# Rotary heads of a float32 network: queries stacked as a high and a low part on 128 partitions, masked scores by two rounded products

## The chip, the cores and the metric

The kernel runs on one core of one Trainium2 chip, as one launch. The metric is the device time of that core in microseconds (us). Three runs of the kernel before took 1568.48, 1573.48 and 1576.81 us; their median, 1573.48 us, is the time before.

## The reference, cut to what matters

A network of four layers over 256 tokens of 1024 features, all in float32. The last two layers hold the attentions with rotary embedding that the change is about:

- In the third layer eight heads of 64 features attend in a window of 128 tokens (`sliding_window_sink_attention`). Their eight queries share two heads of keys, four queries to a head, and both queries and keys are rotated (`apply_rope`). A second set of eight heads (`forgetting_attention`) is not rotated.
- In the fourth layer sixteen rotated heads share four rotated heads of keys (`dsa_attention`). Each query attends to the 64 keys that an index of eight small heads scores highest; the index has rotated queries and one rotated key head of its own.

```python
def apply_rope(t, cos, sin):
    half = t.shape[-1] // 2
    tf = t.astype(jnp.float32)
    t1, t2 = tf[..., :half], tf[..., half:]
    return jnp.concatenate([t1 * cos - t2 * sin, t2 * cos + t1 * sin], axis=-1).astype(t.dtype)
...
        s = jnp.einsum('bqhgd,bqthd->bhgqt', qi, ks, preferred_element_type=jnp.float32) * scale
        s = jnp.where(sel_valid[:, None, None], s, -jnp.inf)
        p = jax.nn.softmax(s, axis=-1)
        o = jnp.einsum('bhgqt,bqthd->bqhgd', p.astype(v.dtype), vs)
```

## The kernel before, in words

The 256 tokens are two tiles of 128, called m = 0 and m = 1. Nearly all products are of a split form: a float32 number is written as a rounded float32r number (high part, by ACT, L260 for weights) plus the rounded rest (low part, by DVE, L261), and `mm3` (L276 to L279) adds three rounded products of 128 rows, high by high, high by low and low by high. Weights are loaded from HBM by SP's queue into four buffers `raw` (L235), split into the buffers `wh` and `wl`, and used by `tok_out` (L368, tokens on the partitions of the result) or `feat_unit` (L384, features on them).

The stages run in the order of `todo` (L1371): gMLP, FFN, chunk attention, FFN, `even_mix` (L901), its FFN, `dsa` (L1020), mixture of experts. Within and across these the tile framework places the instructions on the queues of the engines, so that products of the next part stand between the small steps of an attention. Each engine then works its queue in that order. The order in `dsa` is set by the string `ORD = "cq0123"` (L44): c is `choose` (L1042), the selection of keys for both token tiles; q is the second half of the queries (`query(1)`, L1081); 0 to 3 are the four groups of four heads (`group`, L1090). `query(0)` and the products for values stand ahead of these. Groups 0 and 1 take their sums from the four PSUM buffers `d`, groups 2 and 3 from the two buffers `m` (L1107).

`attend` (L666) handles a group of four heads. It has four chains, one for each token tile and each pair of heads, and `together` issues their steps in turn. A chain does: the scores of two heads into one PSUM buffer (L678 to L682), the largest of a row (DVE, L697 or L700), the exponential with its sum (ACT, L709, into a buffer `s2`, of which there are four), the transposes (PE, L716), the copy of these (ACT, L719), the product with the values (PE, L724) and the division (DVE, L728, L729). Keys reach to the end of the query's own tile, so a head has 128 keys for m = 0 and 256 for m = 1. For the rotated heads the mask is added by the tensor engine: a rounded product of 128 rows of the identity with the mask (L681) opens the sum, and the score (L682), one float32 product over the 64 features of the head, closes it. Each L682 appears in the profile as two instructions. Heads that are not rotated have no L681; their bias is added by DVE.

`rotate` (L831) makes the rotary embedding of a tile of tokens on DVE: a product with the cosine (L837), two with the sine (L838, L839) and the sum (L841, or L845 twice with the heads of the keys doubled), in buffers `rt`. `tr_copy` (L848) transposes the result, 128 columns at a time (PE, L853), and copies it out (ACT, L854). Two heads lie in each block of 128 columns, so an even head ends on partitions 0 to 63 and an odd head on 64 to 127 (`half`, L736); keys are doubled so that both find them. `ev_sq` (L924) and `ev_kv` (L912) do this in `even_mix`, `ev_iq`, `ev_ki` and `ev_q` (L1030, L1035, L1084) in `dsa`.

`keep` buffers that matter here: six of `a8` and two of `xn`, each given out in turn. `fox_bias` (L965) loads a small table into an `xn` buffer (L968).

Of the kernel before, what the change touches and what calls it, by code (L numbers as in the profile page):

```python
# [16 lines left out]
P = 128  # L17
# [31 lines left out]
# ---------------------------------------------------------------- layouts  # L49


def _rows(w, kk):
    """[K, N] -> [K/(128*kk), 128, kk*N]: row-chunk units, kk chunks of 128 rows each."""
    K, N = w.shape
    return w.reshape(K // (P * kk), kk, P, N).transpose(0, 2, 1, 3).reshape(K // (P * kk), P, kk * N)


def _a_units(w, cols=256):
    """[1024, N] -> [N/cols, 128, 8*cols]: all of K for a block of columns."""
    K, N = w.shape  # L60
    return w.reshape(K // P, P, N // cols, cols).transpose(2, 1, 0, 3).reshape(N // cols, P, (K // P) * cols)


def _b_units(w, cols=512):
    """[1024, N] -> [(N/cols)*2, 128, 4*cols]: half of K for a block of columns."""
    K, N = w.shape
    return (w.reshape(2, K // (2 * P), P, N // cols, cols).transpose(3, 0, 2, 1, 4)
            .reshape((N // cols) * 2, P, (K // (2 * P)) * cols))


def _fm(v):
    """vector [n*128] -> [128, n], entry n*128+p at (p, n)."""
    return v.reshape(-1, P).T
# [5 lines left out]
def _layout(i):  # L79
# [46 lines left out]
    # small vectors, feature-major, side by side  # L126
# [13 lines left out]
    # small vectors, one row  # L140
# [3 lines left out]
    # constants of the shapes alone  # L144
# [14 lines left out]
def tile_net(ctx: ExitStack, tc: tile.TileContext, a: dict, out: bass.AP):  # L159
# [36 lines left out]
    def xn_():  # L196
        return t_keep("xn", D, 2)
# [4 lines left out]
    # ------------------------------------------------------------ constants  # L202
# [29 lines left out]
    # ------------------------------------------------------------ weights  # L232
# [31 lines left out]
    def unit(src, k, where=None, loaded=None):  # L264
        """a unit of k chunks of 128 rows -> for each chunk its two parts [128, columns]."""
# [22 lines left out]
    def together(*chains):  # L288
        """issue the steps of independent chains in turn"""
# [4 lines left out]
    # ------------------------------------------------------------ norms  # L294
# [54 lines left out]
    def norm(m, outs, r=None):  # L349
        """token tile m of the norms outs: (xh, xl, gain row) or (xh, xl, A, B), feature-major"""  # L350
# [33 lines left out]
    def feat_unit(xt, w, psx=None):  # L384
        """feature-major product of one unit of 256 columns -> psum [128, 2, 256]."""
# [8 lines left out]
    def feat_tile(xt, w, ps, m, psx):  # L394
        """token tile m of feat_unit, token-major first."""
# [10 lines left out]
    def feat_pair(xt, ws, psx):  # L406
        """feat_unit of the units ws, one token tile after the other."""
# [25 lines left out]
    def add_rows(d, th, tl, w, first, last, ms=(0, 1), cs=(0, 1)):  # L433
        """one chunk of 128 rows of a down projection into the four sums d[m][c]."""
# [5 lines left out]
    def finish(d, tail, g=None):  # L440
        """the chunks of the tail, one token tile after the other, then h += (g *) sums and its squares."""
# [15 lines left out]
    def out_proj(oT, src, g=None, order=(0, 1, 2, 3)):  # L457
        """h += (g *) o @ w for oT = (oh, ol) feature-major; two chunks of rows per unit."""
# [13 lines left out]
    # ------------------------------------------------------------ modulation  # L472
# [11 lines left out]
    def ada_step(n=1):  # L484
        """the next 256 entries of a modulation: their columns of the weights lie on the partitions"""
# [16 lines left out]
    def mod_scale(nm, i, gain):  # L502
        """(1 + sc) * gain, feature-major."""
# [4 lines left out]
    def spread(v):  # L508
        """feature-major [128, 8] -> [128, 1024], the same row on every partition."""
# [10 lines left out]
    # ------------------------------------------------------------ gated MLPs  # L520
# [69 lines left out]
    # ------------------------------------------------------------ gMLP mixer  # L590
# [74 lines left out]
    # ------------------------------------------------------------ softmax attention  # L665
    def attend(q, kT, vv, mask, oT, g, psx, sinks=None, cumq=None, rmask=None):  # L666
        """heads 4g..4g+3 of 16: q(h) and kT(h) feature-major [64, 256], vv(h, kb) [128, 64], mask(m, pair)
        added to the scores, or rmask(m) by the tensor engine; the result feature-major in oT."""
        ob = g2().rearrange("p m (h d) -> p m h d", h=4)

        def chain(m, hh):
            nk = (m + 1) * P
            ms = slice(m * P, (m + 1) * P)
# [4 lines left out]
            for i, hd in enumerate(pair):  # L678
# [3 lines left out]
                PE.matmul(ps[:, sl], q(hd)[:, ms], kT(hd)[:, 0:nk], start=rmask is None, stop=True)  # L682
# [56 lines left out]
    # ------------------------------------------------------------ chunk attention  # L739
# [17 lines left out]
    def chunk_attn():  # L757
        xk, xq = ahead[2]
        oT = new_xt()
        for j in range(4):  # L760
# [19 lines left out]
            def mask(m, pair):  # L780
# [3 lines left out]
            attend(lambda hd: half(qT, hd - 4 * j), lambda hd: half(kT, hd - 4 * j),  # L784
                   lambda hd, kb: vv[:, kb, (hd - 4 * j) * 64:(hd - 4 * j + 1) * 64], mask, oT, j,
# [45 lines left out]
    def rotate(ps, m, nh, dup=1):  # L831
        """rotary embedding of token-major heads [128, nh*64], each written dup times."""
        n = nh * 64
        t1, t2, o = (t_part("rt", 512, lay["rt"])[:, 0:w] for w in (n, n, n * dup))
# [5 lines left out]
        if dup == 1:  # L840
# [7 lines left out]
    def tr_copy(src, dst, m, scale=1.0):  # L848
        """token-major [128, n*128] -> dst [128, n, 256] at token tile m."""
# [7 lines left out]
    # ------------------------------------------------------------ even layer  # L857
# [21 lines left out]
    def x0_norm(m, gain, xs, rs):  # L879
        """h = x0, the normed h, and its own norm."""  # L880
# [20 lines left out]
    def even_mix():  # L901
        xt = ahead[2]
        kvb = a8()
        skT = kvb[:, 0:512].rearrange("p (k t) -> p k t", k=2)
        sv = kvb[:, 512:768].rearrange("p (m d) -> p m d", m=2)
        lf = kvb[:, 768:784].rearrange("p (m d) -> p m d", m=2)
        cum = kvb[:, 784:800].rearrange("p (m d) -> p m d", m=2)
        sqT = kvb[:, 1024:2048].rearrange("p (k t) -> p k t", k=4)
# [3 lines left out]
        def ev_kv(m, c, ps):  # L912
            tr_copy(rotate(ps[:, 0:128], m, 2, dup=2), skT, m)
# [10 lines left out]
        def ev_sq(m, c, ps):  # L924
            tr_copy(rotate(ps, m, 8), sqT, m, scale=0.125)
# [15 lines left out]
        fv = a8()[:, 0:1024].rearrange("p (m d) -> p m d", m=2)  # L941
# [23 lines left out]
        def fox_bias(j):  # L965
            """for the heads of group j, minus the sums of the keys' columns, causal"""
# [17 lines left out]
        def fox(j, cbs):  # L984
# [6 lines left out]
            attend(lambda hd: half(fqT, hd - 4 * j), lambda hd: half(fkT, hd - 4 * j),  # L991
# [408 lines left out]
```

## Time and profile before

| | us |
|---|---|
| median of three runs | 1573.48 |
| the three runs | 1568.48, 1573.48, 1576.81 |
| span of the profiled execution, first to last instruction | 1564.6 |
| PE busy in it | 1503.8 |
| DVE busy | 1206.7 |
| ACT busy | 940.9 |

The table holds the times and the first part of the page. The profiled execution has no time of its own on record beside its span; what lies around the span (launch and end) is in the runs' times and not in the span, and the median is 8.9 us above it. Starts of instructions are in us from the beginning of the span. A matmul's shown duration runs to the end of its pipeline, and one begins while the last one ends; what a stream of them costs is read from start to start. PEclk 1.00 is 2.4 GHz and 0.50 is 1.2 GHz; a mean between the two is a mixture.

### The profile page before, as it was taken

The page shows a single profiled execution, that of the slowest core. Times are in us where ns is not written, and L with a number is a line of the kernel's source. Part 1 is how long each engine was busy: PE and PEld are TensorE (multiplying, and loading weights), DVE is VectorE, ACT ScalarE, POOL GpSimd, SP SyncE. Part 2 cuts the span into 40 slices and gives each one's busy share as a digit, 9 for nine tenths or more (in the row PEclk, how much of TensorE's full clock was granted, in tenths as well). Part 3 has the DMA queues.
Part 4 walks back from the last instruction along what each step waited for, and adds up shares of the span by engine and source line. Part 5 has one row for each costly group of instructions (what it writes and reads, how often), then busy time and mean ns, then how long its engine had stood idle before and what let it go on. Part 6 is the DMA issues. An engine that isn't in the chain of part 4 may idle for free. (4 is left out here: it accounts for less than half of the span.)

```text
span 1564.6 us, 23309 instructions
## 1 busy us (share of the span) xinstructions
PE 1503.8 (96%) x9000; PEld 1307.1 (84%) x9000; DVE 1206.7 (77%) x2039; ACT 940.9 (60%) x1567; POOL 15.6 (1%) x26
## 2 busy tenths in 40 slices
PE   6999999999999999999899999999899999999996
PEld 5888998899799898878799997867688888888875
DVE  6688877765798887846888866844688888888996
ACT  7565555565575555645644444535487777777774
POOL 0000000000000000000000000000000000000000
PEclk9999999999999999989999999959899999999998
DMA  8567676364388662532698961510379998899894
GB/s 312 207 226 285 238 249 218 126 233 142 137 314 282 232 240 83 204 120 82 219 356 311 335 226 44 186 54 28 121 274 334 336 334 310 327 349 331 288 354 152
DMA packets 54150, 359.85 MB, mean 230 GB/s; under 512 B 6400, under 2 KB 6656, under 8 KB 15632
## 3 DMA queue, kind: packets, MB, share of 16 engines
q1 hardware_dynamic: 54032, 358.30, 63.6%
q8 instruction: 72, 1.18, 0.3%
q14 instruction: 46, 0.38, 0.1%
HBM read 357.23 MB, written 1.05 MB: 229 GB/s over the span
## 5 line engine op out<-in xcount | busy, mean ns | idle before, releaser
L261 DVE TENSOR_TENSOR wl<-raw,wh 128x1024 fp32r<-128x1024 f32 (+4 forms) x342 | 363.7, 1070 | 85.2 <-ACT wh L260 83.8
L260 ACT ACTIVATE wh<-raw 128x1024 fp32r<-128x1024 f32 (+4 forms) x342 | 315.1, 932 | 145.0 <-DMA raw<-in_fin_dram 41.0
L261 DVE TENSOR_TENSOR wlx<-raw,whx 128x1024 fp32r<-128x1024 f32 (+2 forms) x231 | 258.7, 1123 | 44.1 <-ACT whx L260 43.2
L260 ACT ACTIVATE whx<-raw 128x1024 fp32r<-128x1024 f32 (+2 forms) x231 | 224.2, 976 | 51.4 <-PE m L278 14.7
L277 PE MATMUL d<-wh,a 128*128 128x512 f32 (+4 forms) x448 | 167.7, 376 | 6.1 <-ACT a L343 6.1
L278 PE MATMUL d<-wl,a 128*128 128x512 f32 (+4 forms) x448 | 167.0, 374 | 0.9 <-DVE wl L261 0.9
L279 PE MATMUL d<-wh,a 128*128 128x512 f32 (+4 forms) x448 | 166.0, 371 | 0.2 <-DVE a L346 0.2
L278 PE MATMUL m<-a,wh 128*128 128x256 f32 x496 | 142.5, 287 | 0.0
L277 PE MATMUL m<-a,wh 128*128 128x256 f32 x496 | 141.9, 286 | 0.0
L279 PE MATMUL m<-a,wl 128*128 128x256 f32 x496 | 141.7, 286 | 0.0
L492 DVE SCALAR_TENSOR_TENSOR raw<-raw,silu_c 128x1024 f32<-128x1024 f32 x96 | 116.1, 1219 | 6.2 <-DMA raw<-in_e_ada_dram 2.9
L277 PE MATMUL d<-a,th 128*128 128x512 f32 x264 | 106.6, 404 | 2.8 <-ACT th L549 2.8
L278 PE MATMUL d<-a,th 128*128 128x512 f32 x264 | 104.4, 396 | 0.0
L277 PEld LDWEIGHTS d<-wh,a 128*128 128x128 f32 x448 | 86.4, 193 | 20.2 <-ACT a L343 8.3
L278 PE MATMUL d<-wlx,a 128*128 128x512 f32 (+2 forms) x272 | 100.2, 369 | 1.1 <-DVE wlx L261 1.1
L277 PE MATMUL d<-whx,a 128*128 128x512 f32 (+2 forms) x272 | 99.4, 366 | 0.6 <-ACT a L653 0.6
L279 PE MATMUL d<-whx,a 128*128 128x512 f32 (+2 forms) x272 | 99.1, 364 | 0.0
L279 PE MATMUL d<-a,tl 128*128 128x512 f32 x264 | 97.8, 397 | 0.9 <-DVE tl L550 0.9
L278 PEld LDWEIGHTS d<-wl,a 128*128 128x128 f32 x448 | 86.4, 193 | 14.0 <-DVE wl L261 2.2
L279 PEld LDWEIGHTS d<-wh,a 128*128 128x128 f32 x448 | 86.2, 192 | 13.9 <-DVE a L346 1.9
L278 PEld LDWEIGHTS m<-a,wh 128*128 128x128 f32 x496 | 95.7, 193 | 1.8 <-issue 0.7
L277 PEld LDWEIGHTS m<-a,wh 128*128 128x128 f32 x496 | 95.4, 192 | 1.2
(354 smaller groups left out, 3507.3 us busy)
## 6 DMA issues: line engine op xcount, KB each, us to landing
raw<-in_fin_dram SPq DMA_DIRECT2D x66, 1024.0 KB, 5.3
raw<-in_x_dn_dram SPq DMA_DIRECT2D x40, 1024.0 KB, 5.7
raw<-in_fdn_dram SPq DMA_DIRECT2D x33, 1024.0 KB, 6.4
raw<-in_x_gate_dram SPq DMA_DIRECT2D x32, 1024.0 KB, 6.3
raw<-in_x_up_dram SPq DMA_DIRECT2D x32, 1024.0 KB, 6.8
raw<-in_e_ada_dram SPq DMA_DIRECT2D x24, 1024.0 KB, 5.3
raw<-in_o_ada_dram SPq DMA_DIRECT2D x24, 1024.0 KB, 6.8
raw<-in_wo_dram SPq DMA_DIRECT2D x16, 1024.0 KB, 5.0
```

The source lines that it names most:

```text
L260: S.activation(hi[:, cs], r[:, cs], AF.Copy)
L261: V.tensor_tensor(lo[:, cs], r[:, cs], hi[:, cs], op=ALU.subtract)
L277: PE.matmul(ps, lh, rh, start=start, stop=False)
L278: PE.matmul(ps, lh, rl, start=False, stop=False)
L279: PE.matmul(ps, ll, rh, start=False, stop=stop)
L492: V.scalar_tensor_tensor(rr, rr, 1.0, silu_c, op0=ALU.mult, op1=ALU.mult, accum_out=t[:, i:i + 1])
```

## The change

For the rotated queries, `rotate` gives two parts: the sum is rounded by ACT into the first 64 columns of a head's block of 128 and the rest is put by DVE into the other 64. `stack` transposes these blocks, so that a head's query has its high part on partitions 0 to 63 and its low part on 64 to 127. Keys stay doubled; `stack` rounds them and also keeps their low part (`kh`, `kl`). A score is then two rounded products over 128 rows, the stacked query with `kh` and with `kl`, behind the same mask product. Queries of the index, heads without rotation and the chunk attention keep their form. The buffers move: the stacked query parts lie in `s2` before they are transposed; in `even_mix` the rounded keys take an `xn` buffer, the stacked queries an `a8` one; in `dsa` the first queries take both `xn` buffers and the second two new buffers `qs`. The diff also drops comments; those hunks are left out here.

```diff
-    def attend(q, kT, vv, mask, oT, g, psx, sinks=None, cumq=None, rmask=None):
+    def attend(qk, vv, mask, oT, g, psx, sinks=None, cumq=None, rmask=None):
...
-                PE.matmul(ps[:, sl], q(hd)[:, ms], kT(hd)[:, 0:nk], start=rmask is None, stop=True)
+                ops = qk(hd, m)
+                for n, (q, k) in enumerate(ops):
+                    PE.matmul(ps[:, sl], q, k, start=rmask is None and n == 0, stop=n == len(ops) - 1)
...
+    def halves(qT, kT, h0):
+
+        return lambda hd, m: [(half(qT, hd - h0)[:, m * P:(m + 1) * P], half(kT, hd - h0)[:, 0:(m + 1) * P])]
+
+    def stacked(Q, kh, kl, h0, kv):
+
+
+        def ops(hd, m):
+            q = Q[(hd - h0) // 4][:, hd % 4, m * P:(m + 1) * P]
+            return [(q, k[:, kv(hd), 0:(m + 1) * P]) for k in (kh, kl)]
+
+        return ops
+
+    def stack(src, m, dst, low=None, scale=1.0):
+
+
+        n = src.shape[1] // P
+        ps = pst()
+        for i in range(n):
+            PE.transpose(ps[:, i * P:(i + 1) * P], src[:, i * P:(i + 1) * P], ident)
+        p3 = ps[:, 0:n * P].rearrange("p (k t) -> p k t", k=n)
+        at = lambda t: t[:, :, m * P:(m + 1) * P]
+        S.activation(at(dst), p3, AF.Copy, scale=scale)
+        if low is not None:
+            V.tensor_tensor(at(low), p3, at(dst), op=ALU.subtract)
...
-    def rotate(ps, m, nh, dup=1):
-        """rotary embedding of token-major heads [128, nh*64], each written dup times."""
+    def rotate(ps, m, nh, dup=1, parts=False):
...
-        t1, t2, o = (t_part("rt", 512, lay["rt"])[:, 0:w] for w in (n, n, n * dup))
+        t1, t2 = (t_part("rt", 512, lay["rt"])[:, 0:n] for _ in range(2))
+        o = None if parts else t_part("rt", 512, lay["rt"])[:, 0:n * dup]
...
-        if dup == 1:
+        if parts:
+            V.tensor_tensor(t1, t1, t2, op=ALU.add)
+            o = []
+            for h0 in range(0, nh, 4):
+                o.append(t_part("s2", 512, 4))
+                o4 = o[-1].rearrange("p (h r d) -> p h r d", h=4, r=2)
+                S.activation(o4[:, :, 0, :].bitcast(F32R), hv(t1)[:, h0:h0 + 4, :], AF.Copy)
+                V.tensor_tensor(o4[:, :, 1, :], hv(t1)[:, h0:h0 + 4, :], o4[:, :, 0, :], op=ALU.subtract)
+        elif dup == 1:
...
-        kvb = a8()
-        skT = kvb[:, 0:512].rearrange("p (k t) -> p k t", k=2)
...
+        sk = xn_(F32R).rearrange("p (r k t) -> p r k t", r=2, k=2)
+        skh, skl = sk[:, 0], sk[:, 1]
+        sqs = a8(F32R).rearrange("p (g k t) -> p g k t", g=2, k=4)
+        sqs = [sqs[:, g] for g in range(2)]
...
-            tr_copy(rotate(ps[:, 0:128], m, 2, dup=2), skT, m)
+            stack(rotate(ps[:, 0:128], m, 2, dup=2), m, skh, skl)
...
-            tr_copy(rotate(ps, m, 8), sqT, m, scale=0.125)
+            for o, q in zip(rotate(ps, m, 8, parts=True), sqs):
+                stack(o, m, q, scale=0.125)
...
-            attend(lambda hd: half(sqT, hd - 8), lambda hd: half(skT, hd, g),
-                   lambda hd, kb: sv[:, kb, g * 64:(g + 1) * 64], None, oT, 2 + g, psd, rmask=mask_swa,
+            attend(stacked(sqs, skh, skl, 8, lambda hd: g), lambda hd, kb: sv[:, kb, g * 64:(g + 1) * 64], None, oT, 2 + g, psd, rmask=mask_swa,
...
-            tr_copy(rotate(ps[:, 0:256], m, 4, dup=2), kT, m)
+            stack(rotate(ps[:, 0:256], m, 4, dup=2), m, kh, kl)
...
-            qT = t_part("rb", D, 2).rearrange("p (k t) -> p k t", k=4)
+            for _ in range(2):
+                q = xn_(F32R) if c == 0 else t_part("qs", D, 2, F32R)
+                qs.append(q.rearrange("p (k t) -> p k t", k=4))
...
-                tr_copy(rotate(ps, m, 8), qT, m, scale=0.125)
+                for o, q in zip(rotate(ps, m, 8, parts=True), qs[2 * c:]):
+                    stack(o, m, q, scale=0.125)
...
-            attend(lambda hd: half(qT, hd - h8), lambda hd: half(kT, hd, g),
-                   lambda hd, kb: vv[:, kb, g * 64:(g + 1) * 64],
+            attend(stacked(qs, kh, kl, 0, lambda hd: g), lambda hd, kb: vv[:, kb, g * 64:(g + 1) * 64],
```

## Rows read from the trace of the kernel before

**Rows 1.** The page's first line: the span of the profiled execution.
```profile
span 1564.6 us, 23309 instructions
```

**Rows 2.** Busy time by stretch: us; PE, PEld, DVE, ACT, POOL (instructions); PEclk; DMA share, GB/s.
```profile
618.00:659.00 41.00, 37.57 (x253) 32.70 (x252) 33.90 (x80) 27.74 (x51) 1.12 (x3) 1.00 0.47 164
659.00:666.55 7.55, 7.55 (x25) 4.21 (x24) 4.06 (x13) 3.26 (x12) 0.00 (x0) 0.84 0.62 234
666.55:684.04 17.49, 17.49 (x89) 14.75 (x89) 9.61 (x31) 8.42 (x20) 0.00 (x0) 0.88 0.46 151
684.04:692.30 8.26, 8.26 (x26) 4.42 (x24) 4.58 (x15) 3.89 (x15) 0.00 (x0) 0.74 0.54 190
692.30:700.00 7.70, 7.70 (x59) 7.70 (x58) 2.76 (x14) 3.21 (x11) 0.00 (x0) 0.84 0.00 0
1000.00:1018.50 18.50, 17.89 (x105) 14.82 (x103) 18.03 (x67) 9.79 (x16) 0.00 (x0) 1.00 0.23 85
1020.20:1061.80 41.60, 41.48 (x146) 30.08 (x147) 17.10 (x42) 14.78 (x53) 0.00 (x0) 0.55 0.15 51
1061.80:1090.00 28.20, 28.14 (x156) 20.51 (x154) 11.23 (x29) 12.79 (x39) 0.00 (x0) 1.00 0.11 38
```

**Rows 3.** Timeline of PE, masked scores of the third layer: start, us, instruction.
```profile
659.01 0.33 PE L681 MATMUL d<-masks_r 128*128 128x128 f32 x1
659.27 0.48 PE L682 MATMUL d<-a 64*128 64x128 f32 x2
659.68 0.33 PE L681 MATMUL d<-masks_r 128*128 128x128 f32 x1
...
661.69 0.39 PE L681 MATMUL d<-masks_r 128*128 128x256 f32 x1
662.01 0.70 PE L682 MATMUL d<-a 64*128 64x256 f32 x2
662.64 0.39 PE L681 MATMUL d<-masks_r 128*128 128x256 f32 x1
```

**Rows 4.** Timeline of PE, scores of heads that are not rotated.
```profile
704.07 1.18 PE L682 MATMUL d<-g,g 64*128 64x256 f32 x8
705.18 0.58 PE L278 MATMUL m<-a,wh 128*128 128x256 f32 x1
```

**Rows 5.** Timeline of PE, rounded products of 128 rows, at 2.4 GHz, then at 1.2 GHz.
```profile
62.11 0.28 PE L278 MATMUL m<-a,wh 128*128 128x256 f32 x1
62.23 0.28 PE L279 MATMUL m<-a,wl 128*128 128x256 f32 x1
...
62.63 0.27 PE L277 MATMUL m<-wh,a 128*128 128x128 f32 x1
62.74 0.27 PE L278 MATMUL m<-wl,a 128*128 128x128 f32 x1
...
693.00 0.41 PE L278 MATMUL m<-a,wh 128*128 128x256 f32 x1
693.21 0.41 PE L279 MATMUL m<-a,wl 128*128 128x256 f32 x1
```

**Rows 6.** Timeline of PE, the transposes of a rotated tile.
```profile
974.14 0.60 PE L853 MATMUL t<-cst,rt 128*128 128x128 f32 x4
974.49 0.40 PE L277 MATMUL d<-wh,a 128*128 128x328 f32 x1
```

**Rows 7.** Groups by line and shape, 1015 to 1095 us: busy us, mean ns, idle before.
```profile
L719 ACT ACTIVATE pT<-t 128x256 f32<-128x256 f32 x8 | 3.1, 386 | 4.9 <-PE t L716 4.8
L854 ACT ACTIVATE rb<-t 128x512 f32<-128x512 f32 x2 | 1.2, 597 | 8.4 <-PE t L853 8.4
L346 DVE TENSOR_TENSOR a<-t,a 128x256 fp32r<-128x256 f32 x8 | 3.4, 423 | 4.5 <-ACT a L343 4.5
L841 DVE TENSOR_TENSOR rt<-rt 128x512 f32<-128x512 f32 x2 | 1.4, 676 | 0.0
```

**Rows 8.** Waits, 1015 to 1095 us: us in total, times, longest.
```profile
PE d L681 <- DVE sel L1074: 1.5, 1, 1.5
```

More of the change, by code (lines that the diff above doesn't have):

```diff
@@ L194, in a8, with xn_ @@
         return t_keep("a8", 2048, 6, dt)
-    def xn_():
-        return t_keep("xn", D, 2)
+    def xn_(dt=F32):
+        return t_keep("xn", D, 2, dt)
     def g2(bufs=None):
@@ L672, in chain @@
             nk = (m + 1) * P
-            ms = slice(m * P, (m + 1) * P)
             pair = [4 * g + hh, 4 * g + hh + 2]
@@ L782, in mask @@
                 return rb3[:, i:i + 3:2, :] if m else rb3[:, i:i + 3:2, P:2 * P]
-            attend(lambda hd: half(qT, hd - 4 * j), lambda hd: half(kT, hd - 4 * j),
-                   lambda hd, kb: vv[:, kb, (hd - 4 * j) * 64:(hd - 4 * j + 1) * 64], mask, oT, j,
+            attend(halves(qT, kT, 4 * j), lambda hd, kb: vv[:, kb, (hd - 4 * j) * 64:(hd - 4 * j + 1) * 64], mask, oT, j,
                    psd if j < 3 else psm)
@@ L902, in even_mix @@
         xt = ahead[2]
-        kvb = a8()
-        skT = kvb[:, 0:512].rearrange("p (k t) -> p k t", k=2)
[L905 to L908, printed above, removed]
+        fvb = a8()
+        fv = fvb[:, 0:1024].rearrange("p (m d) -> p m d", m=2)
+        kvs = fvb[:, 1024:1312]
+        sv = kvs[:, 0:256].rearrange("p (m d) -> p m d", m=2)
+        lf = kvs[:, 256:272].rearrange("p (m d) -> p m d", m=2)
+        cum = kvs[:, 272:288].rearrange("p (m d) -> p m d", m=2)
+        sk = xn_(F32R).rearrange("p (r k t) -> p r k t", r=2, k=2)
+        skh, skl = sk[:, 0], sk[:, 1]
+        sqs = a8(F32R).rearrange("p (g k t) -> p g k t", g=2, k=4)
+        sqs = [sqs[:, g] for g in range(2)]
         cumT = keep.tile([8, T], F32, name="cumT")
@@ L936, in swa @@
         def swa(g):
-            attend(lambda hd: half(sqT, hd - 8), lambda hd: half(skT, hd, g),
-                   lambda hd, kb: sv[:, kb, g * 64:(g + 1) * 64], None, oT, 2 + g, psd, rmask=mask_swa,
+            attend(stacked(sqs, skh, skl, 8, lambda hd: g), lambda hd, kb: sv[:, kb, g * 64:(g + 1) * 64], None, oT, 2 + g, psd, rmask=mask_swa,
                    sinks=lambda pair: sinks[:, pair[0] - 8:pair[0] - 5:2])
-        fv = a8()[:, 0:1024].rearrange("p (m d) -> p m d", m=2)
         fT = []
@@ L989, in mask @@
                 return cb[:, P:3 * P] if m else cb[:, 0:P]
-            attend(lambda hd: half(fqT, hd - 4 * j), lambda hd: half(fkT, hd - 4 * j),
-                   lambda hd, kb: fv[:, kb, hd * 64:(hd + 1) * 64], mask, oT, j, psd if j == 0 else psm,
+            attend(halves(fqT, fkT, 4 * j), lambda hd, kb: fv[:, kb, hd * 64:(hd + 1) * 64], mask, oT, j, psd if j == 0 else psm,
                    cumq=lambda m, hd: cum[:, m, hd:hd + 1])
@@ L1021, in dsa @@
         xt = ahead[2]
-        ib, kvb = a8(), a8()
+        ib, kk = a8(), a8(F32R)
         oT = new_xt()
@@ L1027, in dsa @@
         sel = t_part("sel", 512, 1, F32R).rearrange("p (m t) -> p m t", m=2)
-        kT = kvb[:, 0:1024].rearrange("p (k t) -> p k t", k=4)
-        vv = kvb[:, 1024:1536].rearrange("p (m d) -> p m d", m=2)
+        kh, kl = (kk[:, i * D:(i + 1) * D].rearrange("p (k t) -> p k t", k=4) for i in range(2))
+        vv = ib[:, 1536:2048].rearrange("p (m d) -> p m d", m=2)
         def ev_iq(m, c, ps):
@@ L1081, in query @@
         def query(c, ready=()):
-            qT = t_part("rb", D, 2).rearrange("p (k t) -> p k t", k=4)
+            for _ in range(2):
+                q = xn_(F32R) if c == 0 else t_part("qs", D, 2, F32R)
+                qs.append(q.rearrange("p (k t) -> p k t", k=4))
             def ev_q(m, _, ps):
-                tr_copy(rotate(ps, m, 8), qT, m, scale=0.125)
+                for o, q in zip(rotate(ps, m, 8, parts=True), qs[2 * c:]):
+                    stack(o, m, q, scale=0.125)
             tok_out(xt, a["o_q"][2 * c:2 * c + 2], 512, ev_q, psm, ready=ready)
-            qs.append(qT)
         def group(g, psx):
-            qT, h8 = qs[g // 2], 8 * (g // 2)
-            attend(lambda hd: half(qT, hd - h8), lambda hd: half(kT, hd, g),
-                   lambda hd, kb: vv[:, kb, g * 64:(g + 1) * 64],
+            attend(stacked(qs, kh, kl, 0, lambda hd: g), lambda hd, kb: vv[:, kb, g * 64:(g + 1) * 64],
                    None, oT, g, psx,
```

## The prediction, made before the changed kernel ran

> **What bounds the kernel now.** I read the page's span first: 1564.6 us [rows 1], 8.9 us below the median of the runs; all sums below are differences, made in the span and then taken from the median. Next the busy time by stretch [rows 2], at the places where rotated heads attend. The reader is to see that PE has no free time there (7.55 of 7.55 us, 8.26 of 8.26, 41.48 of 41.60, 28.14 of 28.20) while DVE and ACT are busy for about half or less. So in these stretches the queue of PE sets the end, and what PE is spared is gained, until DVE or ACT set it. The same rows show the second point: the granted clock is 0.84 and 0.74 in the two stretches of masked scores of the third layer and 0.55 over 41.60 us of the fourth. Between the levels of 1.2 and 2.4 GHz a mean of 0.55 is (1 - 0.55) / 0.5 = 90% of the time at 1.2 GHz. In the third layer it falls while PE issues masked scores without a pause; in the fourth it falls when PE has waited 1.5 us for the selection [rows 8] and then issues masked scores.
>
> Last the timeline of PE, from start to start. A masked head costs 0.67 us with 128 keys (659.01 to 659.68) and 0.95 us with 256 (661.69 to 662.64) at 2.4 GHz [rows 3]. Without a mask product between them, eight instructions of the same 64-row kind, which are four heads of 256 keys, take 1.11 us [rows 4], 0.28 a head. So float32 alone isn't the dear part; its turns with the 128-row mask product are. Rounded products of 128 rows, one behind the other, start every 0.12 us with 256 columns, 0.11 with 128, and 0.21 at 1.2 GHz [rows 5].
>
> **The change, part by part.** There are six groups, two in the third layer and four in the fourth, each with four heads of 128 keys and four of 256.
>
> *Scores.* A head becomes three rounded 128-row products in a row. I take the pitch of rows 5: 0.33 and 0.36 us, a group 4 x 0.33 + 4 x 0.36 = 2.76 us. That price isn't in the trace for this very sequence; its nearest row below is the same 0.11 and 0.12 (nothing makes it cheaper than the stream of `mm3`), above it is the pitch behind a mask product today, 0.26 and 0.32 [rows 3], that is 0.78 and 0.96 a head and no gain at all. I take the lower, since `mm3` has the same types, rows and an own weight load per product. Third layer: 7.55 + 8.26 us of scores [rows 2] become 5.5, **-10.3 us**. Other products stand ready behind them on PE, so this is gained in full.
>
> *Clock behind the scores, third layer.* Of the next stretches (1 - 0.88) / 0.5 x 17.49 = 4.2 us and (1 - 0.84) / 0.5 x 7.70 = 2.5 us are at 1.2 GHz [rows 2]. If the clock no longer falls, half of 6.7 is gained: **-3.3 us**. Ends: 0 and -3.3. I take the gain, since streams of rounded 128-row products stand at 1.00 in 618 to 659.
>
> *Fourth layer, groups 0 and 1 (1020.2 to 1061.8).* 41.60 us at a mean of 0.55 are 22.9 us of work at 2.4 GHz. Twenty heads are scored in it (groups 0 and 1, and the 128-key heads of group 2): 8 x 0.95 + 12 x 0.67 = 15.6 us, so 7.3 us are transposes and value products. After: 8 x 0.36 + 12 x 0.33 = 6.8, with the 7.3, 14.1 us at 2.4 GHz, 28 us at 1.2. PE isn't alone then. ACT has 14.78 us in the stretch [rows 2] and gets four rounded halves of 0.39 and two more copies of 0.60 [rows 7], 17.5; DVE has 17.10 and gets four subtractions of 0.42, 18.8. The steps of a chain hand over between the three, and one wait is new: the query halves of `query(1)` now lie in the four buffers `s2`, which the exponentials of group 0 also want, so ACT's first exponential waits for transposes of a rotation that DVE does after the selection. Ends: 19 us (DVE alone) and 28 us plus some 2 of hand-overs. Without a reason for either end I take 25: **-16.6 us**.
>
> *Fourth layer, groups 2 and 3 (1061.8 to 1090).* Clock 1.00, PE full. Eight heads of 256 keys and four of 128: 8 x 0.59 + 4 x 0.34 = 6.1 us less. I take **-5.5**, as DVE and ACT (11.23 and 12.79 of 28.20) are late next.
>
> *Transposes.* A tile of eight queries has eight blocks of 128 columns instead of four; three such sets on two tiles: 24 more, at 0.35 / 4 = 0.09 us [rows 6]: **+2.1 us** on PE, which is full.
>
> *ACT and DVE ahead of the scores.* Per tile ACT gets 2 x 0.39 + 0.60 = 1.4 us and DVE 2 x 0.42 = 0.8 (rows 7: copy and subtraction of 256 columns, copy of 512). Third layer, two tiles, with two subtractions for the keys: 2.5 us of DVE in 618 to 659, where it is busy 33.90 of 41.00 and PE already lacks 3.4 us. What hides it is the queue of products ready for PE; **+1.0**, ends 0 and 2.5. Fourth layer: the keys' two subtractions of 0.68 lie before 1000 us, where no selection runs yet; the first queries' four (1.7 us) stand on DVE right before the selection, where DVE is busy 18.03 of 18.50 us, and PE waits for its end [rows 8]. **+1.7**, ends 0 and 3.1 with the keys.
>
> *Buffers and loads.* The rounded keys hold one of two `xn`, so the load of the second bias table (L968) waits on SP's queue for the last scores of `swa(1)`, and weight loads behind it wait too. Its table is needed only by `fox_bias(1)`, after group `fox(0)` and the products of `fox_in(1)`: 0. If that cover were gone, it would be the load's own time plus the weights behind it. `a8` stays at six, `rt` loses users: 0.
>
> Sum: -10.3 - 3.3 - 16.6 - 5.5 + 2.1 + 1.0 + 1.7 = **-30.9 us**: span 1533.7, median 1573.5 - 30.9 = 1542.6, say **1543 us**. Later stages start earlier by that much and are unchanged.
>
> **Rivals.**
> *A: the clock stays as low as now.* Then a third-layer group costs 24 products x 0.21 = 5.0 us, -5.7 for both, nothing behind them; the long stretch 28 + 2 us, -11.6. With -5.5 and +4.8: -18.0, 1555 us. For it: PE's wait for the selection stays and grows, and the transposes and value products around the scores are the same. Against: the scores were most of the work at the low level and become a dense stream.
> *B: the weight load of each product shows (slower).* Heads cost 0.78 and 0.96: 24 x 0.11 + 24 x 0.01 = +2.9 us, the clock as before, +4.8 for transposes, ACT and DVE: +7.7, 1581 us. It decides where the second product of a head starts 0.20 us or more after the first. For it: rows 3, where each product behind the mask shows 0.26 or 0.32. Against: rows 5. The Trainium skill, page "TensorE: Matmul & The Clock Gate", section "Part 3: Packing small matmuls — row/col tiling", says that a weight load overlaps running matmuls only when it goes to another group of rows; by that rule alone the new 128-row products would be those of this rival. By that rule the trace doesn't go: its 128-row products, each with a load, start every 0.12 us.
> *C: the waits eat the long stretch.* ACT's queue works in order; if its exponentials stand behind the late query halves, and the selection is later still, 1020.2 to 1061.8 keeps its 41.6 us and the third layer's clock still falls: -10.3 - 5.5 + 4.8 = -11.0, 1562 us, and a little more waiting makes it no change. For it: ACT waited 8.4 us for the copies of `query(1)` [rows 7] in just this place. Against: those waits were for PE, which gets faster.
>
> **How the numbers follow.** Forecast 0.76, A 0.14, C 0.06, B 0.04. A measurement of this kernel tells about 0.5% (7.9 us) from no change. The forecast and A lie beyond it, C half: faster 0.92; the other half of C and a part of B: same 0.05; slower 0.03. Range: the low ends of all terms are -10.3 - 3.3 - 22.6 - 6.1 + 2.1 = -40.2, 1533, and 4 us for the spread of the runs: 1529. Upwards it takes in A and the same spread: 1560. Outside are B, C's larger part and a gain beyond all my bounds, some 0.15.
>
> **What would show it.** Right: in the groups of rotated heads no 64-row product; three 128-row products in a row 0.11 to 0.12 us apart; swa groups of some 2.8 us each; a clock at 1.00 around them; 24 more transposes; the stretch of groups 0 and 1 between 20 and 30 us; PE's wait for the selection about 3 us. Wrong: a pitch of 0.2 or more at 2.4 GHz (B), a clock of 0.5 from the selection to group 2 (A), ACT idle before the exponentials of group 0 with `s2` as the cause (C), or a PE that waits in the FFN or the experts for what it had ready before.

## The result, and the profile after

The kernel after takes 1546.59 us (median of four runs, 1544.33 to 1550.23), the one before 1570.98 beside it (four runs, 1568.06 to 1576.81): a ratio of 0.9845, 95% interval 0.9823 to 0.9868, or 24.4 us less. Forecast were 1543 us and 30.9 less. The profiled executions have spans of 1545.8 and 1564.6 us [rows 1], 18.8 apart. The two differences don't contradict each other. A run's time is 2.1 us longer than its span (1547.93 and 1545.8 us for the profiled run after), so the medians are spans of 1568.9 and 1544.5: the profiled execution before was 4.3 us below its median, the one after 1.3 above. Of the 8.9 us between span and median before, only some 2 lie around the span. Lines of `attend` have moved: L684 is the score, L699 the largest of a row, L711 the exponential, L718 its transposes, L721 their copy, L726 the value product; L760 and L763 are the transposes and the copy of `stack`, L875 and L876 the halves of the queries.

PE, kernel after, scores of `swa(0)`, start to start (as [rows 3]):

```profile
659.99 0.33 PE L681 MATMUL d<-masks_r 128*128 128x128 f32 x1
660.15 0.38 PE L684 MATMUL d<-xn,a 128*128 128x128 f32 x2
660.38 0.27 PE L681 MATMUL d<-masks_r 128*128 128x128 f32 x1
...
661.78 0.28 PE L681 MATMUL d<-masks_r 128*128 128x256 f32 x1
661.90 0.40 PE L684 MATMUL d<-xn,a 128*128 128x256 f32 x2
662.14 0.28 PE L681 MATMUL d<-masks_r 128*128 128x256 f32 x1
...
662.84 0.40 PE L277 MATMUL m<-wh,a 128*128 128x512 f32 x1
```

A head costs 0.33 us with 128 keys (660.38 to 660.71, the next mask) and 0.36 with 256 (661.78 to 662.14), against 0.67 and 0.95. Busy time by stretch, kernel after (as [rows 2]): the two groups of scores with what follows each, groups 0 and 1 of the fourth layer, groups 2 and 3:

```profile
core 0: us, PE busy (x) PEld busy (x) DVE busy (x) ACT busy (x) POOL busy (x), PEclk, DMA share, GB/s
...
659.99:662.84 2.85, 2.85 (x25) 2.85 (x25) 2.85 (x6) 0.27 (x1) 0.00 (x0) 1.00 0.83 336
662.84:682.72 19.88, 17.27 (x90) 14.35 (x89) 10.96 (x40) 11.16 (x31) 0.00 (x0) 0.91 0.56 184
682.72:685.50 2.78, 2.78 (x25) 2.72 (x23) 2.54 (x3) 1.54 (x2) 0.00 (x0) 1.00 0.47 197
685.50:700.00 14.50, 13.31 (x87) 10.72 (x86) 8.85 (x41) 7.87 (x32) 0.00 (x0) 0.92 0.22 76
...
1009.90:1045.30 35.40, 29.76 (x166) 27.00 (x166) 20.06 (x49) 18.14 (x60) 0.00 (x0) 0.76 0.25 90
1045.30:1067.30 22.00, 21.16 (x148) 17.75 (x148) 9.82 (x27) 12.68 (x39) 0.00 (x0) 1.00 0.01 1
```

The third layer's scores are as forecast, at 1.00. Behind them PE now stands still (a bracket gives the idle time of the engine just before a row, and what ended it), here behind `swa(0)`:

```profile
663.07 0.40 PE L278 MATMUL m<-wl,a 128*128 128x512 f32 x1
666.08 0.33 PE L718 MATMUL t<-cst,s 128*128 128x128 f32 x1 [2.61 <-ACT s L711]
```

The stretch of groups 0 and 1 is not as forecast: 35.4 us where 25 was said, PE idle for 5.6 of them (0.1 before), the clock at 0.76. What PE waits for and what ACT and DVE do there, kernel after, first DVE, then ACT, then PE:

```profile
1012.43 0.42 DVE L699 TENSOR_REDUCE s_nmx<-d 128x2 f32<-128x256 f32 x1
...
1020.09 0.75 DVE L876 TENSOR_TENSOR s<-rt,s 128x256 f32<-128x256 f32 x2
```

```profile
1015.42 1.06 ACT L260 ACTIVATE wh<-raw 128x1024 fp32r<-128x1024 f32 x1 [6.02 <-PE m L279]
1016.74 0.72 ACT L875 ACTIVATE s<-rt 128x256 fp32r<-128x256 f32 x2 [0.26 <-DVE rt L870]
1018.45 1.09 ACT L763 ACTIVATE qs<-t 128x512 fp32r<-128x512 f32 x2 [0.98 <-PE t L760]
1019.42 0.72 ACT L875 ACTIVATE s<-rt 128x256 fp32r<-128x256 f32 x2
1020.16 1.28 ACT L711 ACT_TABLE_LOAD   x1
1021.46 0.37 ACT L711 ACTIVATE s<-d,s_nmx 128x128 f32<-128x128 f32 x1
```

```profile
1017.76 1.09 PE L760 MATMUL t<-cst,s 128*128 128x128 f32 x8
...
1022.46 0.33 PE L718 MATMUL t<-cst,s 128*128 128x128 f32 x1 [0.68 <-ACT qs L763]
1023.29 1.03 PE L718 MATMUL t<-cst,s 128*128 128x128 f32 x3 [0.50 <-ACT s L711]
1026.09 1.97 PE L718 MATMUL t<-cst,s 128*128 128x128 f32 x8 [1.76 <-ACT pT L721]
```

The first maximum of group 0 is done by 1012.9, the first exponential starts at 1021.46, 8.6 us later. ACT is first idle for 2.6 us of this (the end of the 6.02 us before 1015.42), then splits a weight (L260), writes halves of `query(1)` into `s2` (L875), copies their transposes and loads a table (1.28 us). The exponentials stand behind all this in ACT's queue.

Stage by stage the two traces differ like this. "Fourth layer" runs on PE from the first product of the selection's scores (1000.6 before, 990.3 after) to the first product of the spread behind group 3 (L515; 1090.4 and 1069.0). It holds the selection, `query(1)` and all groups, so that it doesn't matter which of them a scheduler puts first. The time at 1.2 GHz in it is from the granted clock that the trace records.

| kernel | fourth layer, us | of it at 1.2 GHz | whole kernel: median, ratio to before, 95% interval |
|---|---|---|---|
| before | 89.9 | 37.5 | 1 |
| after | 78.7 | 17.1 | 1546.6, 0.9845, 0.9823 to 0.9868 |
| e1 masks first | 71.0 | 3.4 | 1538.0, 0.9798, 0.9765 to 0.9831 |
| e2 one float32 product | 77.9 | 13.7 | 1545.2, one run |
| e3 third layer only | 89.8 | 37.5 | 1559.1, 0.9929, 0.9901 to 0.9956 |
| e4 fourth layer only | 78.7 | 17.1 | 1559.6, 0.9931, 0.9909 to 0.9953 |
| e5 mask by pair | 84.9 | 34.1 | 1550.7, one run |
| e6 own halves | 71.1 | 3.4 | 1536.7, 0.9802, 0.9762 to 0.9842 |
| e7 splits ready | 75.7 | 13.7 | 1543.7, 0.9835, 0.9809 to 0.9861 |
| e8 = e6 + e7 | 74.3 | 13.7 | 1542.9, 0.9828, 0.9794 to 0.9862 |
| e9 control of e6 | 78.8 | 17.1 | 1545.9, one run |
| e10 = e6, wide masks | 70.4 | 3.4 | 1538.9, 0.9817, 0.9791 to 0.9843 |
| e11 hybrid | 70.4 | 3.4 | 1540.3, 0.9819, 0.9789 to 0.9849 |
| e12 filled waits | 78.2 | 13.7 | 1546.2, 0.9857, 0.9822 to 0.9891 |

The prediction's terms for this stage, -16.6, -5.5, +1.4 and +1.7, make 70.9 us out of 89.9.

### The profile page after: what moved, and what is told of

Its sections match the earlier page's. It is cut to its first block, busy times and chain, and to the rows that moved or that the text cites. A ratio compares the mean times of both kernels' runs of the same rounds, so it can differ in the third digit from the quotient of the medians.

```text
span 1545.8 us, 23399 instructions
## 1 busy us (share of the span) xinstructions
PE 1475.7 (95%) x9024; PEld 1298.0 (84%) x9024; DVE 1211.3 (78%) x2055; ACT 946.7 (61%) x1585; POOL 15.6 (1%) x26
## 4 chain that ended last, share of the span: by engine, by line
PE 79%; DVE 10%; DMA 5%; ACT 4%; issue 1%; POOL 1%; SPq 0%; POOLq 0%; ACTq 0%; DVEq 0%
PE d L277 11%; PE d L278 11%; PE d L279 11%; PE m L279 9%; PE m L278 9%; PE m L277 9%; DMA raw<-in_fin_dram 3%; PE t L279 2%; PE t L278 2%; PE t L277 2%; PE d L726 2%; DVE wl L261 1%; PE t L322 1%; PE t L718 1%; PE t L1235 1%
## 5 line engine op out<-in xcount | busy, mean ns | idle before, releaser
L260 ACT ACTIVATE wh<-raw 128x1024 fp32r<-128x1024 f32 (+4 forms) x342 | 315.0, 932 | 133.0 <-DMA raw<-in_fin_dram 34.0
L260 ACT ACTIVATE whx<-raw 128x1024 fp32r<-128x1024 f32 (+2 forms) x231 | 224.1, 976 | 64.1 <-PE m L278 21.7
```

The source lines that it names most:

```text
L260: S.activation(hi[:, cs], r[:, cs], AF.Copy)
```

## The experiments

**What made a masked head dear** (e1, e5, e2).

e1, on the kernel before:

```diff
+            if rmask is not None:
+                PE.matmul(two(ps), ident_r, rmask(m).unsqueeze(1).to_broadcast([P, 2, nk]), start=True, stop=False)
+                yield
             for i, hd in enumerate(pair):
                 sl = slice(i * nk, (i + 1) * nk)
-                if rmask is not None:
-                    PE.matmul(ps[:, sl], ident_r, rmask(m), start=True, stop=False)
-                PE.matmul(ps[:, sl], q(hd)[:, ms], kT(hd)[:, 0:nk], start=rmask is None, stop=True)
+                PE.matmul(ps[:, sl], q(hd)[:, ms], kT(hd)[:, 0:nk], start=rmask is None, stop=rmask is None or i == 1)
```

> The kernel before with the 64-row float32 scores kept; only the order of the products of a group is changed: one mask product for both heads of a pair (256 or 512 columns), and the masks of all four chains ahead of the scores. Theory 1 (what made a masked head dear is the turn from the 128-row mask product to the 64-row score and back): with two turns to a group instead of sixteen a third-layer group takes 4 masks of 0.12 and 0.22 us and 8 scores at the pitch of the unmasked ones, 0.28 us for 256 keys and about half for 128, together 2.5 to 3.2 us instead of 7.55 and 8.26; the whole kernel gains 20 to 30 us on the one before, without stacked parts. Theory 2 (the float32 score over 64 rows is dear in itself): a group stays at 6 us or more, and the kernel within 0.5% of the one before.

PE of e1, `swa(0)` (L679 mask, L683 score):

```profile
655.66 0.97 PE L679 MATMUL d<-masks_r 128*128 128x256 f32 x4
656.56 1.68 PE L683 MATMUL d<-a 64*128 64x128 f32 x16
658.17 0.50 PE L277 MATMUL m<-wh,a 128*128 128x512 f32 x1
```

The group takes 2.51 us instead of 7.55 (6.5 at 2.4 GHz), less than the 2.85 of the change. Theory 1 holds, and the whole kernel is 32 us below the one before, more than the 20 to 30 said, with its float32 scores untouched: no halves, no low keys, no added transposes. Groups 0 and 1, which took 41.6 us at 0.55, take 23.1 at 0.93:

```profile
1011.80:1034.90 23.10, 19.23 (x134) 14.84 (x135) 17.02 (x43) 14.01 (x53) 0.00 (x0) 0.93 0.26 92
```

e5, on e1:

```diff
                 PE.matmul(two(ps), ident_r, rmask(m).unsqueeze(1).to_broadcast([P, 2, nk]), start=True, stop=False)
-                yield
```

> As the first run (float32 scores over 64 rows kept), but the mask of a pair stands right ahead of the pair's two scores: eight turns between 128 and 64 rows to a group in place of sixteen (before) or two (first run). If a turn has a price of its own, a third-layer group lies on the line between the two: before 4 x 0.67 + 4 x 0.95 = 6.5 us at 2.4 GHz with sixteen turns, 2.5 us in the first run with two, so 0.28 a turn and 4.2 us here (4.0 to 4.5). Rival (not the number of turns but the mask products that are narrow or twice as many cost): about 2.5 to 3 us here, as the masks are the same as in the first run.

PE of e5, `swa(1)`, and its busy time by stretch:

```profile
678.64 0.71 PE L682 MATMUL d<-a 64*128 64x128 f32 x4
679.28 0.38 PE L679 MATMUL d<-masks_r 128*128 128x256 f32 x1
679.59 0.71 PE L682 MATMUL d<-a 64*128 64x128 f32 x4
680.23 0.49 PE L679 MATMUL d<-masks_r 128*128 128x512 f32 x1
680.65 1.13 PE L682 MATMUL d<-a 64*128 64x256 f32 x4
681.71 0.50 PE L679 MATMUL d<-masks_r 128*128 128x512 f32 x1
```

```profile
678.43:683.20 4.77, 4.77 (x21) 2.93 (x19) 4.18 (x12) 2.58 (x8) 0.00 (x0) 1.00 0.43 136
1010.66:1047.70 37.04, 35.78 (x135) 26.66 (x136) 17.01 (x42) 14.45 (x53) 0.00 (x0) 0.54 0.16 57
```

The same products as in e1 take 4.77 us instead of 2.5, where 4.2 was said. A pair of 128-key heads costs 0.95 us (679.28 to 680.23), one of 256-key heads 1.48 (680.23 to 681.71). Read instruction by instruction, the four scores of a pair start 0.11 us apart with 128 keys and 0.22 with 256; the mask of a pair costs 0.12 and 0.23 where another mask follows it (e1). That leaves 0.39 us in either pair for its two turns. In the kernel before, the same reading leaves 0.34 and 0.39 a head, some 2.9 of the 6.5 us of a group. So turns have nearly one price. What the line between before and e1 missed is something else that e1 does: without masks between them, scores of even heads (partitions 0 to 63) and of odd heads (64 to 127) stand side by side, as the two heads of one chain are both even or both odd, and there they start in pairs 0.01 us apart, eight of 128 keys in 0.55 us and eight of 256 in 1.06. Of the 2.26 us between e5 and e1, six turns are some 1.2 by that price; the rest fits two heads running at once. No run takes this alone. In the fourth layer the clock is at 0.54 again.

e2, on the kernel after:

```diff
-            return [(q, k[:, kv(hd), 0:(m + 1) * P]) for k in (kh, kl)]
+            return [(q.bitcast(F32), kh[:, kv(hd), 0:(m + 1) * P].bitcast(F32))]
```

> The changed kernel, but a score is one float32 product over the 128 stacked rows in place of two rounded ones; the part of the keys' low half is left out. This is float32 behind a 128-row mask product without a change of rows. Theory 1 (the turn between 64 and 128 rows is the price): a head of 256 keys takes about 0.11 for the mask and 0.3 for the score, 0.4 us at 2.4 GHz, a third-layer group below 4 us. Theory 2 (float32 next to a rounded product is the price, whatever the rows): 0.67 and 0.95 us a head as before, a group about 6.5 us at 2.4 GHz.

PE of e2, heads of 256 keys of `swa(0)`:

```profile
661.30 0.47 PE L681 MATMUL d<-masks_r 128*128 128x256 f32 x1
661.61 0.59 PE L684 MATMUL d<-xn,a 128*128 128x256 f32 x2
661.85 0.47 PE L681 MATMUL d<-masks_r 128*128 128x256 f32 x1
```

0.55 us a head, 0.33 with 128 keys, the group some 3.4 us. Without a change of rows, float32 right behind a rounded mask costs 0.55 instead of 0.95 and 0.33 instead of 0.67. Theory 2 falls: the change of rows was the larger part. The type is not free, though: with 256 keys two rounded products, at 0.36 a head, are 0.19 us cheaper.

**Which layer gave what** (e3, e4).

e3 is the kernel after with `dsa` as before:

```diff
-            stack(rotate(ps[:, 0:256], m, 4, dup=2), m, kh, kl)
+            tr_copy(rotate(ps[:, 0:256], m, 4, dup=2), kT, m)
...
-                for o, q in zip(rotate(ps, m, 8, parts=True), qs[2 * c:]):
-                    stack(o, m, q, scale=0.125)
+                tr_copy(rotate(ps, m, 8), qT, m, scale=0.125)
```

e4 is the kernel after with `even_mix` as before:

```diff
-            stack(rotate(ps[:, 0:128], m, 2, dup=2), m, skh, skl)
+            tr_copy(rotate(ps[:, 0:128], m, 2, dup=2), skT, m)
...
-            for o, q in zip(rotate(ps, m, 8, parts=True), sqs):
-                stack(o, m, q, scale=0.125)
+            tr_copy(rotate(ps, m, 8), sqT, m, scale=0.125)
```

> The change in the third layer alone; the fourth layer has its old form. From the starts in the two traces the third layer gave 9 to 10 us of the gain: expected 9 us below the kernel before (ratio 0.994), with the fourth layer's stretch of groups 0 and 1 at 41 to 42 us as before. The prediction's terms for it were -10.3 and -3.3 with +0.7 and +1.0, -11.9 in all. Rival (gains of the third layer are lost again in the FFN behind it, which waits for weights): no difference at the start of the fourth layer.

> The change in the fourth layer alone; the third layer has its old form. From the starts in the two traces: first scores 1 us earlier and groups 0 to 3 with 10 to 12 us less, of which 2 to 3 are lost again at a low clock ahead of the experts: 9 to 12 us below the kernel before (ratio 0.993). If the low clock ahead of the experts is a matter of chance and not of this change, 12 to 14. The prediction's terms for it were -16.6, -5.5, +1.4 and +1.7, -19.0 in all.

The third layer alone gains 11.0 us (1570.1 to 1559.1), the fourth alone 10.5; the sum, 21.5, is within the intervals what both give together. In e3 the fourth layer is unchanged at 89.8 us (89.9 before), in e4 it is as in the change, 78.7. So the third layer's terms (-11.9 in all) fit as a sum, and the fourth's (-19.0) were too large by 8 us. The low clock ahead of the experts follows neither layer's part: 10.2 us before, in e4 and, with the whole change, in e7; 13.7 in e1 and e3; 17.1 after and in e6. Its cause is open.

**Where the fourth layer's gain went** (e6, e9, e7, e8).

e6, on the kernel after; `lay["sh"]` is two buffers of their own in `dsa`, and `s2` in `even_mix`:

```diff
-RT = {"even": 4, "dsa": 5}
+RT = {"even": 4, "dsa": 3}
...
-                o.append(t_part("s2", 512, 4))
+                o.append(t_part(*lay["sh"]))
```

> The changed kernel; in the fourth layer the query halves get two buffers of their own instead of the four that the exponentials use (paid for with two fewer of the buffers of the rotation). Theory (the prediction's rival C in part: the exponentials of group 0 wait for a buffer that holds halves of the late queries): the first exponential comes within 3 us of the first maximum instead of 8.6 us behind it, the stretch from the first score to the last value product of groups 0 and 1 falls from 35.4 us to 29 to 32, the kernel by 3 to 6 us against the changed one. Rival (the low clock of 13.7 us alone made the stretch long, and it comes from PE's wait for the selection): the stretch stays at 34 us or more, the low clock at 10 us or more, the time within 2 us.

ACT of e6 (L712 exponential, L876 halves), and its groups 0 and 1:

```profile
1007.14 1.28 ACT L712 ACT_TABLE_LOAD   x1
1010.63 0.37 ACT L712 ACTIVATE s<-d,s_nmx 128x128 f32<-128x128 f32 x1 [2.20 <-DVE s_nmx L700]
...
1014.37 0.72 ACT L876 ACTIVATE sh<-rt 128x256 fp32r<-128x256 f32 x2 [0.32 <-DVE rt L871]
```

```profile
1007.64:1035.10 27.46, 23.36 (x163) 20.53 (x164) 19.56 (x48) 17.41 (x60) 0.00 (x0) 0.94 0.32 115
```

The first exponential now waits for its maximum alone (2.20, DVE), and stands ahead of the halves; the table load too has moved ahead. The stage falls from 78.7 to 71.1 us, the kernel to 1536.7, which is 7 us below the change by the ratios and 10 by the medians, where 3 to 6 were expected (one of its four runs took 1545.2). The rival falls with it: PE waits 1.4 us for the selection as before, and the time at 1.2 GHz is 3.4 us, not 17.1.

e9, on the kernel after:

```diff
-RT = {"even": 4, "dsa": 5}
+RT = {"even": 4, "dsa": 3}
```

> A control for the sixth run: the changed kernel with three rotation buffers in place of five in the fourth layer and nothing else. If the gain of the sixth run came from the buffers of the halves, here the first exponential stays 8 us or more behind the first maximum, the low clock 10 us or more and the stretch of groups 0 and 1 at 33 us or more. Rival (the gain came from another order of the instructions, set off by the fewer rotation buffers): the stretch at 28 us as in the sixth run.

The first exponential starts 8.8 us behind the first maximum, groups 0 and 1 take 35.2 us, the stage 78.8: nothing of e6's gain is from the rotation buffers.

e7, on the kernel after; e8 is e6 with the same edit:

```diff
-READY = 0
+READY = 2
```

> The changed kernel with two weight units of the second queries split ahead of the selection, so that DVE has no weight split right behind the selection and the ten products that had moved behind the first scores stand ahead of them again. Theory (two weight splits of 1.2 us each, pushed behind the selection by the added DVE work, make the second queries late): selection 1 to 3 us later, stretch of groups 0 and 1 from 35.4 to 27 to 30 us; kernel 2 to 5 us below the changed one. Rival (the stretch is bound by the buffers that halves and exponentials share): stretch shorter only by the 4 us of the ten products, so the kernel the same within 2 us or slower.

> Both edits of the two runs before together. If both causes are real and separate: stretch of groups 0 and 1 at 23 to 27 us, which is the 25 us of the prediction, and the kernel 5 to 10 us below the changed one, 1537 to 1541 us. If only one of them counts: no better than the better of the two.

e7: the selection ends 1.2 us later (20.9 us after the stage's start, not 19.6 or 19.7), and the stage is 3.0 us shorter: the two weight splits behind the selection had a price, and the +1.7 us of DVE work that the prediction charged was real but had been paid by pushing them there. In the whole kernel this gain is within the spread. e8 is a miss. The two gains don't add: 74.3 us, worse than e6 alone. With the ten products of `query(1)` gone from behind the first scores PE stands still for 3.5 us from the first mask to the value products, 1.8 in e6, and 13.7 us at 1.2 GHz are back where e6 had 3.4.

**The clock itself** (e12). Sixteen products that nobody reads, meant for PE's waits of 0.50 and 1.76 us:

```diff
                 PE.transpose(pt[:, b * P:(b + 1) * P], s2[:, b * P:(b + 1) * P], ident)
+            if rmask is not None and sinks is None and g == 0 and m == 0:
+                for _ in range(8):
+                    PE.matmul(ps[:, T:2 * T], ident_r, rmask(1), start=True, stop=True)
```

> The changed kernel with sixteen extra mask products of 256 columns (about 0.12 us each at 2.4 GHz, 2 us in all) that nobody reads, in group 0 of the fourth layer, eight behind the transposes of each of the two first chains, where PE waits 0.5 and 1.76 us for ACT. Theory (the 13.7 us at 1.2 GHz that begin there come from PE standing still so much between the selection and the value products of group 0): with PE busy in these waits the clock stays at 2.4 GHz for all but 3.4 us of the stretch, which falls from 35.0 to 30 to 31 us, and the kernel by 4 to 5 us, in spite of 2 us of useless work. Rival (transposes and value products behind rounded scores run at 1.2 GHz here whatever stood before): low for 13.7 us as before, the stretch at 35 to 36 us, the kernel the same or 1 us slower.

PE of e12 (L721 filler, L729 value products of group 0), and two stretches:

```profile
1022.88 1.20 PE L721 MATMUL d<-sel,masks_r 128*128 128x256 f32 x8
1024.42 1.09 PE L718 MATMUL t<-cst,s 128*128 128x128 f32 x8 [0.33 <-ACT pT L724]
1025.35 2.79 PE L729 MATMUL d<-a,pT 128*128 128x64 f32 x24
1027.97 0.39 PE L322 MATMUL t<-cst,g 128*128 128x128 f32 x2
```

```profile
1020.00:1034.70 14.70, 10.87 (x86) 9.61 (x84) 8.21 (x23) 10.31 (x42) 0.00 (x0) 1.00 0.39 144
1034.70:1045.00 10.30, 10.28 (x44) 9.66 (x45) 2.16 (x8) 3.59 (x13) 0.00 (x0) 0.50 0.01 2
```

Half a hit. The wait of 0.50 us stayed, that of 1.76 became 0.33. With it filled the clock does not fall there: 24 value products take 2.6 us (1025.35 to 1027.97), in the kernel after 5.0. But it falls at 1034.7, behind the next wait (1.84 us, group 1's copies), for 10.2 us, so the stretch is 33.2 us, not 30 to 31, and the kernel the same as the change. Filling one wait handed the low clock to the next. The length of a wait alone does not decide it: at group 1's copies e6 waits 1.85 us and e10 2.06 with no fall behind it.

**Both remedies together** (e10, e11). e10, on e6; e11 is e10 with the edit of e4 and the last two added lines here:

```diff
+            if rmask is not None:
+                PE.matmul(two(ps), ident_r, rmask(m).unsqueeze(1).to_broadcast([P, 2, nk]), start=True, stop=False)
+                if sinks is not None:
+                    yield
...
-                if rmask is not None:
-                    PE.matmul(ps[:, sl], ident_r, rmask(m), start=True, stop=False)
...
```

The last two added lines put the third layer's masks ahead of its scores, as in e1.

> The sixth run with one mask product for both heads of a pair (256 or 512 columns). The masks of two heads of 128 keys cost 0.12 in place of 0.22 us, those of 256 keys the same: 0.2 us a group, 1.2 us in all, if nothing else moves: 1535 us. Rival (a product of 512 columns is as long as two of 256 and the order of the queue changes): the same time as the sixth run within 2 us. Either way it should lie below both kernels.

> The third layer in its old form with the masks ahead of the scores (first run), the fourth as in the run before. This saves in the third layer the halves, the low keys and eight more blocks of transposes: by the trace 2 x 4 x 0.13 us = 1.0 us of PE and 2 to 3 us of DVE and ACT, while a group of scores takes 2.5 us either way. If PE's products for the values cover the extra work there, as the prediction took it up to 1.0 us, the time is the same as the run before within 2 us; if not, 2 to 4 us lower.

Both stages are at 70.4 us, 0.7 below e6, and the kernels within the spread of e6, so e10's expectation is not decided. e11 against e10 shows no gain, as it should be if PE's products cover the third layer's extra halves. e1, e6, e10 and e11 can't be told apart by their intervals. Their ratios lie 4 to 7 us below that of the change (6 to 10 by the medians), and the intervals touch the change's, which was not timed beside them; what is clear is the stage, 70.4 to 71.1 against 78.7 us.

## Why the prediction was right, and where it was off

The time (1543 said, 1546.6 measured) and the direction were right, the time in part by luck. The sum said -30.9; the medians show -24.4 and the two profiled spans -18.8. Of the missing 6.5 us in the medians the kernel before gave back 2.5, as its median fell from 1573.5 to 1571.0 with the fourth run, which leaves the time 4 us off. The third layer gave about what was said as a sum (11.0 by e3, 11.9 said), the fourth 11.2 us where 19.0 were said. By the steps, in the spans:

- *Scores, third layer, -10.3:* 2.85 + 2.78 us after 7.55 + 8.26 make -10.2. The pitch was taken from `mm3`, and the turns were named as the dear part; e1, e2 and e5 show that they are the larger part, 0.34 to 0.39 of 0.67 and 0.95 us a head. The 0.28 us a head of [rows 4] was too low a price for float32 alone: those eight instructions too start in pairs 0.01 us apart, two heads at once, and one head by itself takes 0.43 (e5). Rival B falls: the second product of a head starts 0.11 us after the first. The Trainium skill, page "TensorEngine Tiling (Array Packing)", section "Key Properties", says that changing the tiling mode drains TensorE. The trace of e5 agrees: the two turns of a pair cost 0.39 us beyond its products.
- *Clock behind them, -3.3:* not obtained there. Means of 0.91 over 19.88 us and 0.92 over 14.50 are 3.6 and 2.3 us at 1.2 GHz; 4.2 and 2.5 were there before. What is late next was not asked here: PE now waits 2.61 and 1.19 us for the exponentials of `swa(0)` and `swa(1)`. e1, with cheap scores and no halves, waits 2.09 and 1.06 in the same places, so it is the speed of the scores that lays this bare. A gain of this kind came later and was not forecast: from the end of the scores of `swa(1)` to the fourth layer there are 19.6 us at 1.2 GHz before and 6.8 after, and 308.3 us became 304.8.
- *DVE, ACT and transposes ahead of them, +1.0 and +0.7:* nearly free. From the first rotary product on DVE (L837, now L866) to the first mask of `swa(0)` it is 29.61 us after 29.45.
- *Groups 0 and 1, 41.6 to 25:* the mis-sized term. From the first score to the last value product it is 35.0 us, 4.0 of them the ten products of `query(1)`; 31.0 without them. The text named the new wait ("the query halves of `query(1)` now lie in the four buffers `s2`, which the exponentials of group 0 also want") and then took a middle "without a reason for either end". e6 measures it: 7.6 us of the stage. Of these some 6.9 are the clock, if work at 1.2 GHz takes twice its time: half of the 13.7 us that vanish. It is rival C's wait with rival A's result.
- *Groups 2 and 3, -5.5:* the last value product follows that of group 1 by 21.6 us where it was 27.7, -6.1, the lower bound of the text.
- *Transposes, +2.1:* eight take 1.09 us in the row at 1017.76 above, 0.13 each and not 0.09, so 24 would be 3.1 us. How much of that other waits covered can't be read from these runs.
- *DVE ahead of the selection, +1.7:* 19.6 us after 19.7. It was not free: the scheduler moved two weight splits behind the selection, and e7 puts them back for 1.2 us. PE's wait for the selection, said to be about 3 us, is 1.4.
- *Buffers, 0:* no wait for `xn` or `a8` showed; `s2`, which the text had put under groups 0 and 1 without a price, is the 7.6 us above.
- *Later stages, 0:* from L515 to the first transposes of `tk` in the experts (L1202, now L1241) 39.3 us became 41.9, with a low clock of 17.1 instead of 10.2 us in that region. e7 has the whole change and 10.2 there, so the change alone does not bring it; the cause is open. Behind that place 434.8 us follow 434.9.

Taken off half its time at 1.2 GHz, the fourth layer's stage is 67.5 to 71.4 us in all fourteen kernels (before 89.9 - 18.8 = 71.1, after 78.7 - 8.6 = 70.1, e6 71.1 - 1.7 = 69.4). That is an account and no cause, but it says what separates them: PE's spared work turned into waits for DVE and ACT, and what was gained there is the clock. One fall has a regular place: in the twelve kernels in which PE waits 1.4 to 1.6 us for the selection the clock falls 1.2 to 2.3 us after the first mask, and in e7 and e8, with 0.6 us, it does not. What decides in the end whether a wait makes it fall was not settled: e1 has waits of 1.55, 1.20 and 2.17 us and is at 1.2 GHz for 3.4 us, e12 for 10.2 behind one of 1.84.

## What to carry to other kernels

Before changing the arithmetic of a slow small product, take away what stands between its repetitions: here the masks put first gave at least what two rounded products, halves and extra transposes gave, and they brought heads of both halves of the partitions side by side. When a part gets faster, list who shares its buffers with what comes late, and price that wait by itself; a forecast that names it and then takes the middle has not used it. And a second fix for the same wait can cost: e8 took from PE the work that kept it busy.

## What the runs showed of the hardware that was not expected

- Two turns between 64-row and 128-row products cost 0.34 to 0.39 us (before and e5), more than a mask product (0.11 to 0.23) and about as much as the four score instructions of a pair of 128-key heads (0.45).
- Float32 products over different halves of the partitions start in pairs 0.01 us apart where nothing stands between them (e1, and [rows 4]), which fits two running at once: sixteen score instructions take 1.61 us in e1, with one turn, where their starts in e5 would add up to 2.6.
- With many turns the clock did not come back: behind its fall at the selection it stayed low for 37.5 us with sixteen turns a group, 34.1 with eight (e5) and 3.4 with two (e1), though PE was busy for nearly all of the stretch in the first two. Turns are not its only cause: the change has none in these groups, and 17.1 us.
- Float32 over 128 rows behind a rounded mask costs 0.33 and 0.55 us a head; two rounded products cost 0.33 and 0.36.
